# A two-layer hybrid encoder: tokens laid in blocks of 8 columns, and the wide products of the feed-forward put in front of the narrow ones

## The chip, the cores and the metric

The kernel runs on one core of a Trainium2 chip. The metric is the device time in microseconds, the median of several runs of the same program; beside it there is one profiled execution, whose trace gives start and duration of each instruction. TensorE (PE) makes the matrix products and writes them to PSUM; VectorE (DVE), ScalarE (ACT) and GpSimd (POOL) work on the results; SyncE (SP) and, for a few, GpSimd issue the DMA transfers.

## What is computed

512 tokens of width 1024 lie on a grid of 8 rows and 64 columns. Two layers are applied, then a final RMS norm:

```python
for l in range(DEPTH):                                    # DEPTH = 2
    x = x + hybrid_mixer(rms_norm(x, norm_mix[l]), ...)   # neighbourhood attention || grouped-query attention
    x = x + memory_cross_attention(rms_norm(x, ...), rms_norm(mem, ...), ...)
    x = x + conv_ffn(rms_norm(x, norm_ffn[l]), w_up[l], conv_w[l], conv_b[l], w_down[l])
return rms_norm(x, norm_final)

def conv_ffn(h, w_up, conv_w, conv_b, w_down):
    u = h @ w_up                                          # (512, 2 * 2816)
    up = jnp.pad(u, ((0, 0), (1, 1), (0, 0)))
    u = up[:, :-2] * conv_w[0] + up[:, 1:-1] * conv_w[1] + up[:, 2:] * conv_w[2] + conv_b
    gate, val = jnp.split(u, 2, axis=-1)
    return (jax.nn.silu(gate) * val) @ w_down
```

The neighbourhood attention looks at a window of all 8 rows by 16 columns around each token. The convolution of the feed-forward, in contrast, runs over the tokens in their natural order, which is row by row: token n stands in row n // 64 and column n % 64, and its neighbours are tokens n - 1 and n + 1.

## The kernel before, in words

**Layout.** The activations are held transposed, as eight tiles xT[0..7] of 128 channels by 512 tokens, in fp32. The host lays the tokens out column by column (position = column * 8 + row), so that a window of columns is a run of positions. Every matrix product is computed in parts: an operand is split into hi (rounded to the product's format) and lo (the rest), and a product is made of hi x hi, hi x lo and lo x hi (mm3, L925). gemm_T (L931) sums such triples over the 128-row chunks of the contraction; each single product is one PE.matmul at L101 (a counting wrapper), so all of them have this line in the profile.

**Stages of a layer.** Input projection and both attentions are woven together (weave and Filler), then come the output projection, the memory attention and the feed-forward. A Norm object closes a stage: close (L1017) adds the product in PSUM to xT[c], copies the sum back to xT[c], writes hi of the next operand from PSUM (operand, L1025), then lo, then the square for the norm's statistic (L1034). The statistic becomes a row of factors that is spread over the partitions by four small products (row_bank, L991) and copied to the tile rep (row_rep, L998).

**The feed-forward.** The 22 units of 128 gate and 128 value channels are worked through in the order of sequence() (L836), which interleaves the units with rows of the down projection of the group before (GROUPS holds 6, 6, 5 and 5 units; PLAIN is 6).
- Units 0 to 5 are plain: up_project (L1843, up_first L1848 for the first ones) makes 24 products of 512 columns for each side, gate and value, from the operand tiles of the norm, ffn.ops; up_finish (L1869) multiplies by rep and calls convolve.
- Units 6 to 21 use a two-by-two fast multiplication with fewer block products. scale_tokens (L1908) makes the normalised tokens xn with one DVE instruction for each xT[c]; token_sums and split_form (L1915, L1930) make seven forms of 4 x 256 columns, hi and lo side by side in 512. up_forms (L1945) calls product() (L1952) seven times for a unit. A call makes, for each of four chunks, one product of the weight's hi with hi and lo together (512 columns, "wide") and one of the weight's lo with hi alone (256 columns, "narrow"):

```python
for k in range(4):
    i = 4 * part + k
    both = xform[form][k // 2][:, k % 2]
    PE.matmul(bank, wh[:, i], both, ...)
    PE.matmul(bank[:, halves[0]], wl[:, i], both[:, halves[0]], ...)
```

- convolve (L1874) makes the middle tap and the bias on ACT, then the outer taps on DVE (L1891). In the column order, the neighbour of a token lies 8 positions away, except that the neighbour of the last column lies at the start of the next row; so each outer tap is two instructions, one over 504 columns and one over 7. SiLU, the product of gate and value and the split into hi and lo follow.
- down (L1993) adds a row of the down projection to xT[m] (L1999). After the last group, down_closing (L2001) closes into the first norm of the next layer, or down_last (L2018) ends the kernel: the last group's first two units are added to xT[m] at L2028, and of the rest one half of the tokens is finished transposed and the other half in rows of tokens.

**The order of the work.** SP's transfers keep the order in which the program writes them. The instructions of PE, ACT, DVE and POOL are put into a new order by a planner (Order, L347): it simulates the program with written-down costs for each instruction (Step.times, L300) and buffer counts (SLOTS, L199), gives every instruction a due time from the products that need it, replays the order several times with random delays and keeps the best of 12 rounds; the random numbers have a fixed seed. A change of any instruction anywhere can so change the order of others in the whole kernel.

Of the kernel before, what the change touches and what calls it, by code (L numbers as in the profile page):

```python
# [11 lines left out]
F32 = mybir.dt.float32  # L12
F32R = mybir.dt.float32r
AF = mybir.ActivationFunctionType
# [5 lines left out]
P = 128  # L20
# [3 lines left out]
GW = 64  # L24
ROWS = 8
NB = S // P
KC = D // P
HD = 64
MEMN = 256
# [61 lines left out]
class Counted(Free):  # L91
# [4 lines left out]
    def matmul(self, out, lhsT, rhs, **k):  # L96
        n = 1
        for d in rhs.shape[1:]:
            n *= d
        self.ns += max(107.0, (n + 32) / 2.4)  # L100
        return self.engine.matmul(out, lhsT, rhs, **k)  # L101


class PartsView:
# [579 lines left out]
def encoder_kernel(ctx: ExitStack, tc: tile.TileContext, t: dict, out: bass.AP):  # L684
# [151 lines left out]
    def sequence():  # L836

        before = None  # L840
        for g, (j0, nj) in enumerate(GROUPS):
            row = 0
            for j in range(j0, j0 + nj):
                to = 0 if g == 0 else min(KC, 2 * (j - j0) + 1) if j < j0 + nj - 1 else KC
                rows, row = range(row, to), to
                if j < PLAIN:
                    yield "up", j, None
                    continue
                yield "gate", j, None
                if before is not None:  # L850
                    yield "val", before, None
                yield "sums", j, None
                if len(rows) > 1:
                    yield "down", g - 1, rows[:1]
                    rows = rows[1:]
                yield "diffs", j, None
                before = j
                if j == NF - 1:
                    yield "val", j, None
                if rows:  # L860
                    yield "down", g - 1, rows
# [133 lines left out]
                      start=True, stop=True)  # L995
        return pr

    def row_rep(rstd, n, tag, bufs, copy):  # L998

        pr = row_bank(rstd, n)  # L1000
        rep = tpool.tile([P, n * P], F32, tag=tag, name=nm(tag), bufs=bufs)
        copy(rep, pr[:, : n * P])
        return rep, pr[:, : n * P]

    class Norm:
# [8 lines left out]
        def gain(self, c):  # L1014
            return par[:, self.l, self.gcol + c : self.gcol + c + 1]

        def close(self, c, pm):  # L1017


            DVE.tensor_add(pm, pm, xT[c])  # L1020
            DVE.tensor_copy(xT[c], pm)
            self.operand(c, src=pm)
            self.square(c)

        def operand(self, c, act=ACT, src=None, dve=DVE, hi_only=False, lo_only=False):  # L1025
            src = xT[c] if src is None else src
            g = self.gain(c)
            hi, lo = self.ops[c]
            e = None if lo_only else act.activation(hi, src, AF.Copy, scale=g)
            if not hi_only:  # L1030
                dve.scalar_tensor_tensor(lo, src, g, f(hi), op0=ALU.mult, op1=ALU.subtract)
            return e
# [39 lines left out]
            POOL.tensor_tensor(self.rstd, v, mhalf[:, :nb], op=ALU.pow)  # L1072

        def spread(self, copy=ACT.copy):
            self.rep, self.psum = row_rep(self.rstd, self.n // P, "rep", 1, copy)

    def split_psum(hi, lo, ps, scale=None):
        if scale is None:
# [119 lines left out]
    for l in range(DEPTH):  # L1198
# [639 lines left out]


        ffn = nn  # L1840
        acts = {}

        def up_project(j, side):  # L1843
            pm = ps_s() if side else ps_mm()
            gemm_T(pm, get_w(("up", j, side)), ffn.ops, range(KC), 0, KC - 1)
            return pm

        def up_first():  # L1848


            ws, us = [], []
            for side in range(2):
                ws.append(get_w(("up", 0, side)))
                us.append(ps_mm())
                gemm_T(us[side], ws[side], ffn.ops, range(KC - 1), 0, KC - 1)
            for side in range(2):
                gemm_T(us[side], ws[side], ffn.ops, [KC - 1], 0, KC - 1)
                if side == 0:
                    ffn.stat()
            us1 = [up_project(1, 0)]  # L1860
            ffn.spread()
            up_finish(0, us)
            us1.append(up_project(1, 1))
            up_finish(1, us1)
# [9 lines left out]
        def convolve(j, us):  # L1874
            cs = []
            for side in range(2):
                ch = side * NF + j
                u = us[side]
                if side and j >= PLAIN:
                    w = [minus[:, l, i, j : j + 1] for i in range(3)]  # L1880
                else:
                    w = [par[:, l, CW + i * 2 * NF + ch : CW + i * 2 * NF + ch + 1] for i in range(3)]
                cc = tmp()
                ACT.activation(cc, u, AF.Identity, bias=par[:, l, CB + ch : CB + ch + 1], scale=w[1])
                for wi, dst, src in (
                    (w[0], slice(8, S), slice(0, S - 8)),
                    (w[0], slice(1, 8), slice(S - 8, S - 1)),
                    (w[2], slice(0, S - 8), slice(8, S)),
                    (w[2], slice(S - 8, S - 1), slice(1, 8)),
                ):  # L1890
                    DVE.scalar_tensor_tensor(cc[:, dst], u[:, src], wi, cc[:, dst], op0=ALU.mult, op1=ALU.add)  # L1891
                cs.append(cc)
            ACT.activation(us[0], cs[0], AF.Silu)
            DVE.tensor_mul(us[0], us[0], cs[1])
            acts[j] = rpair()
            split_psum(*acts[j], us[0])
            if j == NF - 1 and l + 1 < DEPTH:
                turn_table(AF.Exp)
# [9 lines left out]
        def scale_tokens():  # L1908


            xn.extend(rtile((2, S), F32) for _ in range(4))
            for c in range(KC):
                DVE.scalar_tensor_tensor(xn[c // 2][:, c % 2], xT[c], ffn.gain(c), ffn.psum, op0=ALU.mult, op1=ALU.mult)

        def token_sums():  # L1915

# [28 lines left out]
        def up_forms(j):  # L1945
# [6 lines left out]
            def product(bank, name, part, form, start=True):  # L1952
                if name not in ws:
                    ws[name] = get_w((name, j))
                wh, wl = ws[name]
                for k in range(4):
                    i = 4 * part + k
                    both = xform[form][k // 2][:, k % 2]
                    PE.matmul(bank, wh[:, i], both, start=start and k == 0, stop=False, skip_group_check=True)
                    PE.matmul(bank[:, halves[0]], wl[:, i], both[:, halves[0]], start=False, stop=k == 3, skip_group_check=True)  # L1960

            def total(dst, bank):
                DVE.tensor_reduce(dst, bank.rearrange("p (n c) -> p c n", n=2), axis=AX.X, op=ALU.add)  # L1963
# [29 lines left out]
        def down(g, rows):  # L1993
            j0, nj = GROUPS[g]
            ops = [acts[j] for j in range(j0, j0 + nj)]
            for m in rows:
                pm = ps_mm()
                gemm_T(pm, get_w(("down", g, m)), ops, range(nj), 0, nj - 1)
                DVE.tensor_add(xT[m], xT[m], pm)  # L1999

        def down_closing(g):  # L2001
            j0, nj = GROUPS[g]
            ops = [acts.pop(j) for j in range(j0, j0 + nj)]
            opened = []
            for m in range(KC):
                if m < 3:
                    opened.append((ps_mm(), get_w(("down", g, m))))
                    gemm_T(*opened[m], ops, range(nj - 1), 0, nj - 1)
            for m in range(KC):
                if m < 3:  # L2010
                    pm, w = opened[m]
                    gemm_T(pm, w, ops, [nj - 1], 0, nj - 1)
                else:
                    pm = ps_mm()
                    gemm_T(pm, get_w(("down", g, m)), ops, range(nj), 0, nj - 1)
                nn.close(m, pm)

        def down_last():  # L2018

            parts = [{j: acts.pop(j) for j in range(j0, j0 + nj)} for j0, nj in LAST]  # L2020
            gain = rtile((2, S), F32)
            SP.dma_start(gain, t["gain"])
            for m in range(KC):
                if m % 2 == 0:
                    w = get_w(("down", "a", m // 2))
                pm = ps_mm()
                gemm_T(pm, w, list(parts[0].values()), range(LAST[0][1]), 0, LAST[0][1] - 1, slice(P * (m % 2), P * (m % 2) + P))
                DVE.tensor_add(xT[m], xT[m], pm)  # L2028

            js, ws = list(parts[1]), {}  # L2030

# [115 lines left out]
def _rope_tables():  # L2147


    tok = np.arange(S)  # L2150
    col, row = tok // ROWS, tok % ROWS
    pos = np.stack([row, col], axis=-1).astype(np.float32)
    nf = HD // 4
    inv = np.float32(10000.0) ** (-np.arange(nf, dtype=np.float32) / np.float32(nf))
# [13 lines left out]
def _bias_index():  # L2168


    q = np.arange(P)
    k = np.arange(256)
    ro = (k % ROWS)[None, :] - (q % ROWS)[:, None] + ROWS - 1
    ci = np.empty((P, 3, 256), np.int64)
    for y, (q0, k0) in enumerate(((0, 0), (16, 8), (48, 32))):
        qc, kc = q0 + q // ROWS, k0 + k // ROWS
        s0 = np.clip(qc - 8, 0, GW - 16)[:, None]
        dc = kc[None, :] - qc[:, None]
        ci[:, y] = np.where((kc >= s0) & (kc < s0 + 16), dc + 15, 31)
    return np.broadcast_to(ro[:, None, :], ci.shape), ci  # L2180


# [41 lines left out]
```

## Time and profile before

| what | us |
|---|---|
| median of 3 runs | 1304.17 (1303.88 to 1304.24) |
| the profiled execution's own time | 1304.26 |
| its span, first to last instruction | 1302.5 |
| DVE busy | 916.0 |
| ACT busy | 776.6 |
| POOL busy | 857.7 |

An engine's busy time is the union of its instructions' times. A row of a group reads: line, engine, operation, the names out<-in, partitions x elements and type, count, then the busy time in us and the mean of one in ns, then the engine's idle time just before them and what ended it. A row of the timeline reads: start in us, us, engine, line, operation, names, shape, count of merged instructions. In the chain of waits a piece reads: start in us, us, engine and line, count. In the table of waits: who waited for whom, then us in total, times, and the longest. The durations of TensorE's products overlap; the time from start to start is what a product costs in a stream.

### The profile page before, as it was taken

To read this page: it belongs to the slowest core of one execution; us is meant where nothing else is said; L and a number is where in the kernel's file an instruction comes from. 1 tells how busy PE (TensorE), PEld (TensorE's weight loads), DVE (VectorE), ACT (ScalarE), POOL (GpSimd) and SP (SyncE) were. 2 spreads that over 40 slices of the span, in tenths; PEclk is the share of its full clock that TensorE was granted. 3 is DMA by queue.
4 is the path that set the end of the run, shared out by engine and by line. 5 is a ranking of instruction groups with operands and counts; after the bars stand their busy time and mean duration, and the time that the engine had idled before them with its cause. 6 is when DMAs were issued, how large, how long until landed. Compare 5 with 4: busy or idle time off the path is not lost.

```text
span 1302.5 us, 19581 instructions
## 1 busy us (share of the span) xinstructions
PE 1292.3 (99%) x6699; PEld 1096.4 (84%) x6699; DVE 916.0 (70%) x1869; ACT 776.6 (60%) x1463; POOL 857.7 (66%) x650
## 2 busy tenths in 40 slices
PE   9999999999999999999999999999999999999997
PEld 8888888888888888888888888888888888888887
DVE  6559877665996685676735698776759966666675
ACT  6667866565564554454636687775645545545454
POOL 3657966728667776776746579766466766767673
PEclk9999999999999999999999999999999999999999
DMA  9734599597787789687555435986872454555541
GB/s 289 211 108 121 160 262 203 168 211 199 186 192 204 207 230 234 189 234 212 157 152 172 144 84 185 253 191 214 186 170 85 130 158 134 163 157 150 149 138 65
DMA packets 287426, 229.68 MB, mean 176 GB/s; under 512 B 7648, under 2 KB 243680, under 8 KB 287328
## 3 DMA queue, kind: packets, MB, share of 16 engines
q1 hardware_dynamic: 270016, 194.49, 49.7%
q0 software_dynamic: 16896, 33.56, 14.6%
q8 instruction: 53, 0.87, 0.3%
q10 hardware_dynamic: 416, 0.39, 0.1%
q14 instruction: 45, 0.37, 0.1%
HBM read 218.45 MB, written 69.21 MB: 221 GB/s over the span
## 4 chain that ended last, share of the span: by engine, by line
PE 95%; DVE 3%; ACT 1%; issue 1%; POOL 0%; POOLq 0%; DVEq 0%; ACTq 0%
PE mm L101 69%; PE sc L101 18%; PE tr L101 4%; PE tr L1586 2%; PE tr L1431 1%; PE tr L1780 1%; DVE t L1891 0%; DVE r L1080 0%; DVE sc L1403 0%; PE tr L1501 0%; DVE r L1129 0%; DVE t L1456 0%; DVE t L1489 0%; ACT r L1079 0%; ACT t L1409 0%
## 5 line engine op out<-in xcount | busy, mean ns | idle before, releaser
L790 POOL TENSOR_TENSOR lo<-raw,hi 128x512 fp32r<-128x512 f32 (+3 forms) x325 | 567.0, 1761 | 280.6 <-ACT hi L789 224.1
L789 ACT CAST hi<-raw 128x1024 fp32r<-128x1024 f32 (+3 forms) x361 | 287.8, 814 | 274.4 <-issue 71.3
L101 PE MATMUL mm<-r,hi 128*128 128x512 f32 (+1 forms) x1344 | 432.8, 390 | 0.0
L101 PEld LDWEIGHTS mm<-r,hi 128*128 128x128 f32 x1344 | 246.4, 188 | 49.8
L101 PE MATMUL mm<-r,lo 128*128 128x512 f32 (+1 forms) x832 | 286.5, 347 | 0.0
L101 PE MATMUL mm<-xg,hi 128*128 128x512 f32 x800 | 262.2, 394 | 0.6 <-DVE t L1963 0.6
L101 PE MATMUL mm<-xg,lo 128*128 128x512 f32 (+1 forms) x528 | 177.9, 337 | 0.0
L101 PEld LDWEIGHTS mm<-r,lo 128*128 128x128 f32 x832 | 156.4, 188 | 22.6 <-POOL lo L790 0.5
L101 PEld LDWEIGHTS mm<-xg,hi 128*128 128x128 f32 x800 | 148.6, 188 | 31.9 <-DVE t L1963 1.0
L101 PE MATMUL sc<-xg,hi 128*128 128x512 f32 x352 | 116.3, 395 | 0.0
L101 PE MATMUL mm<-hi,xg 128*128 128x512 f32 (+1 forms) x384 | 111.2, 360 | 0.0
L101 PEld LDWEIGHTS mm<-xg,lo 128*128 128x128 f32 x528 | 99.4, 188 | 12.2
L1086 POOL TENSOR_SCALAR t<-t,s 128x512 f32<-128x512 f32 (+1 forms) x112 | 67.2, 623 | 45.6 <-DVE s L1570 22.2
L101 PE MATMUL sc<-xg,lo 128*128 128x256 f32 (+1 forms) x240 | 79.4, 332 | 0.0
L1982 POOL TENSOR_TENSOR t<-t 128x256 f32<-128x256 f32 x32 | 42.4, 1324 | 56.1 <-ACT t L1981 55.2
L101 PEld LDWEIGHTS sc<-xg,hi 128*128 128x128 f32 x352 | 66.1, 189 | 14.5 <-ACT xg L78 0.4
L101 PEld LDWEIGHTS mm<-hi,xg 128*128 128x128 f32 x384 | 68.0, 189 | 9.1 <-DVE r L1280 0.2
L101 PE MATMUL sc<-r,r 128*128 128x256 f32 (+1 forms) x352 | 74.4, 330 | 0.0
L1989 DVE TENSOR_TENSOR sc<-mm,t 128x256 f32<-128x256 f32 x32 | 13.8, 433 | 79.2 <-ACT t L1988 79.2
L101 PE MATMUL sc<-r,hi 128*128 128x512 f32 x192 | 68.7, 398 | 0.0
L101 PE MATMUL mm<-lo,xg 128*128 128x512 f32 (+1 forms) x192 | 68.6, 357 | 0.0
L790 DVE TENSOR_TENSOR lo<-raw,hi 128x1024 fp32r<-128x1024 f32 (+1 forms) x36 | 44.2, 1229 | 33.8 <-ACT hi L789 33.5
(222 smaller groups left out, 2438.3 us busy)
## 6 DMA issues: line engine op xcount, KB each, us to landing
raw<-in_w_up SPq DMA_DIRECT2D x56, 512.0 KB, 4.5
dr_sums<-in_w_up SPq DMA_DIRECT2D x16, 1024.0 KB, 8.0
dr_diffs<-in_w_up SPq DMA_DIRECT2D x16, 1024.0 KB, 7.6
raw<-dr_sums SPq DMA_DIRECT2D x32, 512.0 KB, 4.1
raw<-dr_diffs SPq DMA_DIRECT2D x32, 512.0 KB, 4.1
raw<-in_w_in SPq DMA_DIRECT2D x25, 512.0 KB, 4.8
raw<-in_w_down SPq DMA_DIRECT2D x32, 384.0 KB, 3.7
raw<-in_w_mem_kv SPq DMA_DIRECT2D x16, 512.0 KB, 4.4
```

The source lines that it names most:

```text
L101: return self.engine.matmul(out, lhsT, rhs, **k)
L789: act.copy(hi[:, k], raw[:, k])
L790: (POOL if eng[0] == "P" else DVE).tensor_sub(lo[:, k], raw[:, k], f(hi)[:, k])
L1086: eng.tensor_scalar(e, e, sums[:, col : col + 1], 1.0, op0=ALU.mult, op1=ALU.mult)
L1431: PE.transpose(tr[:, (2 * i + c) * P : (2 * i + c + 1) * P], es[j][:, i, c * P : (c + 1) * P], ident)
L1586: PE.transpose(tr[:, k * P : (k + 1) * P], es[j][:, k * P : (k + 1) * P], ident)
L1780: PE.transpose(tr[:, (2 * c + i) * P : (2 * c + i + 1) * P], e[:, i, c * P : (c + 1) * P], ident)
L1982: POOL.tensor_add(vc, vc, u2)
L1989: DVE.tensor_add(ch, ah, l4)
```

## The change

1. **Layout.** The host lays the tokens in blocks of 8 columns: position = block * 64 + row * 8 + column in the block. Tables, bias index and the final reshape follow it (host only). The attentions run in this order. 
2. **The feed-forward runs in the natural order.** Two views make the passage between the orders: crossed() reads a row of 512 as 8 x 8 runs of 8 elements in the other order, runs() gives the plain row the same shape. The plain units read hi and lo through crossed() as the moving operand (576 products); the residual adds, the spread of rep, the closes into the next layer and the adds of down_last read one side through crossed(). scale_tokens becomes one ACT and one DVE instruction for each xT[c], and down_last writes its sums to new tiles z.
3. **One instruction for each outer tap**, over 511 columns, in place of two.
4. **In product()** the four wide products come first and the four narrow ones behind them.
5. sequence() can yield down rows for a plain unit.

```diff
+def runs(v):
+    return v.rearrange("p (a b e) -> p a b e", a=GROUPS_OF_COLS, b=ROWS)
+def crossed(v):
+    return v.rearrange("p (a b e) -> p b a e", a=ROWS, b=ROWS)
...
                 if j < PLAIN:
                     yield "up", j, None
+                    if rows:
+                        yield "down", g - 1, rows
                     continue
...
-        copy(rep, pr[:, : n * P])
+        copy(runs(rep), crossed(pr)) if turned else copy(rep, pr[:, : n * P])
...
+            if by_row:
+                DVE.tensor_add(runs(pm), runs(pm), crossed(xT[c]))
+                DVE.tensor_copy(runs(xT[c]), crossed(pm))
+            else:
+                DVE.tensor_add(pm, pm, xT[c])
+                DVE.tensor_copy(xT[c], pm)
+            self.operand(c, src=pm, by_row=by_row)
...
+            if by_row:
+                e = act.activation(runs(hi), crossed(src), AF.Copy, scale=g)
+                src = xT[c]
...
         ffn = nn
+        by_row = [tuple(map(crossed, v)) for v in ffn.ops]
...
-            gemm_T(pm, get_w(("up", j, side)), ffn.ops, range(KC), 0, KC - 1)
+            gemm_T(pm, get_w(("up", j, side)), by_row, range(KC), 0, KC - 1)
...
-                for wi, dst, src in (
-                    (w[0], slice(8, S), slice(0, S - 8)),
-                    (w[0], slice(1, 8), slice(S - 8, S - 1)),
-                    (w[2], slice(0, S - 8), slice(8, S)),
-                    (w[2], slice(S - 8, S - 1), slice(1, 8)),
-                ):
+                for wi, dst, src in ((w[0], slice(1, S), slice(0, S - 1)), (w[2], slice(0, S - 1), slice(1, S))):
                     DVE.scalar_tensor_tensor(cc[:, dst], u[:, src], wi, cc[:, dst], op0=ALU.mult, op1=ALU.add)
...
-                DVE.scalar_tensor_tensor(xn[c // 2][:, c % 2], xT[c], ffn.gain(c), ffn.psum, op0=ALU.mult, op1=ALU.mult)
+                v = xn[c // 2][:, c % 2]
+                ACT.activation(runs(v), crossed(xT[c]), AF.Copy, scale=ffn.gain(c))
+                DVE.tensor_mul(runs(v), runs(v), crossed(ffn.psum))
...
+                both = [xform[form][k // 2][:, k % 2] for k in range(4)]
                 for k in range(4):
-                    i = 4 * part + k
-                    both = xform[form][k // 2][:, k % 2]
-                    PE.matmul(bank, wh[:, i], both, start=start and k == 0, stop=False, skip_group_check=True)
-                    PE.matmul(bank[:, halves[0]], wl[:, i], both[:, halves[0]], start=False, stop=k == 3, skip_group_check=True)
+                    PE.matmul(bank, wh[:, 4 * part + k], both[k], start=start and k == 0, stop=False, skip_group_check=True)
+                for k in range(4):
+                    PE.matmul(bank[:, halves[0]], wl[:, 4 * part + k], both[k][:, halves[0]], start=False, stop=k == 3,
+                              skip_group_check=True)
...
-                DVE.tensor_add(xT[m], xT[m], pm)
+                DVE.tensor_add(runs(xT[m]), runs(xT[m]), crossed(pm))
...
-                nn.close(m, pm)
+                nn.close(m, pm, True)
...
+            z = [v[:, i] for v in (rtile((2, S), F32) for _ in range(4)) for i in range(2)]
...
-                DVE.tensor_add(xT[m], xT[m], pm)
+                DVE.tensor_add(runs(z[m]), crossed(xT[m]), runs(pm))
+                xT[m] = z[m]
...
-    col, row = tok // ROWS, tok % ROWS
+    col, row = tok // GW * ROWS + tok % ROWS, tok // ROWS % ROWS
...
-        "xT": a["x"].reshape(ROWS, GW, D).transpose(2, 1, 0).reshape(D, S),
+        "xT": a["x"].reshape(ROWS, GROUPS_OF_COLS, ROWS, D).transpose(3, 1, 0, 2).reshape(D, S),
```

More of the change, by code (lines that the diff above doesn't have):

```diff
@@ L26 @@
 NB = S // P
+GROUPS_OF_COLS = GW // ROWS
 KC = D // P
@@ L996, in row_bank, with row_rep @@
         return pr
-    def row_rep(rstd, n, tag, bufs, copy):
+    def row_rep(rstd, n, tag, bufs, copy, turned):
         pr = row_bank(rstd, n)
         rep = tpool.tile([P, n * P], F32, tag=tag, name=nm(tag), bufs=bufs)
-        copy(rep, pr[:, : n * P])
+        copy(runs(rep), crossed(pr)) if turned else copy(rep, pr[:, : n * P])
         return rep, pr[:, : n * P]
@@ L1015, in gain, with close, operand @@
             return par[:, self.l, self.gcol + c : self.gcol + c + 1]
[L1017 to L1022, printed above, removed]
+        def close(self, c, pm, by_row=False):
+            if by_row:
[5 more added lines that the diff above has]
+            self.operand(c, src=pm, by_row=by_row)
             self.square(c)
-        def operand(self, c, act=ACT, src=None, dve=DVE, hi_only=False, lo_only=False):
+        def operand(self, c, act=ACT, src=None, dve=DVE, hi_only=False, lo_only=False, by_row=False):
             src = xT[c] if src is None else src
@@ L1028, in operand @@
             hi, lo = self.ops[c]
-            e = None if lo_only else act.activation(hi, src, AF.Copy, scale=g)
+            if by_row:
+                e = act.activation(runs(hi), crossed(src), AF.Copy, scale=g)
+                src = xT[c]
+            else:
+                e = None if lo_only else act.activation(hi, src, AF.Copy, scale=g)
             if not hi_only:
@@ L1074, in spread @@
         def spread(self, copy=ACT.copy):
-            self.rep, self.psum = row_rep(self.rstd, self.n // P, "rep", 1, copy)
+            self.rep, self.psum = row_rep(self.rstd, self.n // P, "rep", 1, copy, self.gcol == G_FFN)
     def split_psum(hi, lo, ps, scale=None):
@@ L1854, in up_first @@
                 us.append(ps_mm())
-                gemm_T(us[side], ws[side], ffn.ops, range(KC - 1), 0, KC - 1)
+                gemm_T(us[side], ws[side], by_row, range(KC - 1), 0, KC - 1)
             for side in range(2):
-                gemm_T(us[side], ws[side], ffn.ops, [KC - 1], 0, KC - 1)
+                gemm_T(us[side], ws[side], by_row, [KC - 1], 0, KC - 1)
                 if side == 0:
@@ L2172, in _bias_index @@
     k = np.arange(256)
-    ro = (k % ROWS)[None, :] - (q % ROWS)[:, None] + ROWS - 1
+    (qr, qc), (kr, kc) = ((v // ROWS % ROWS, v // GW * ROWS + v % ROWS) for v in (q, k))
+    ro = kr[None, :] - qr[:, None] + ROWS - 1
     ci = np.empty((P, 3, 256), np.int64)
     for y, (q0, k0) in enumerate(((0, 0), (16, 8), (48, 32))):
[L2176 to L2179, printed above, removed]
+        s0 = np.clip(q0 + qc - 8, 0, GW - 16)[:, None]
+        dc = k0 + kc[None, :] - (q0 + qc)[:, None]
+        ci[:, y] = np.where((k0 + kc >= s0) & (k0 + kc < s0 + 16), dc + 15, 31)
     return np.broadcast_to(ro[:, None, :], ci.shape), ci
@@ L2222 @@
     y = np.concatenate([y[0].reshape(D, HALF).T, y[1].reshape(HALF, D)])
-    return np.ascontiguousarray(y.reshape(GW, ROWS, D).transpose(1, 0, 2)).reshape(1, S, D)
+    return np.ascontiguousarray(y).reshape(1, S, D)
```

## The prediction

> **What bounds the kernel now.** I read the profile's page first, then the table of what TensorE waited for, then the chain of waits in order of time and the timeline of TensorE, and last the groups of DVE instructions by shape. The profiled execution took 1304.26 us (span 1302.5 us and 1.76 us around it), 0.09 us over the median of the runs, 1304.17 us, so a sum made against it carries over to the median. A measurement of this kernel can tell about 0.2%, 2.6 us, from no change.
>
> ```profile
> PE 1292.3 (99%) x6699; PEld 1096.4 (84%) x6699; DVE 916.0 (70%) x1869; ACT 776.6 (60%) x1463; POOL 857.7 (66%) x650
> PEclk9999999999999999999999999999999999999999
> PE 95%; DVE 3%; ACT 1%; issue 1%; POOL 0%; POOLq 0%; DVEq 0%; ACTq 0%
> ```
> ```profile
> PE tr L101 <- POOL ident masks.py:199: 1.4, 1, 1.4
> PE tr L1431 <- DVE r L1297: 0.8, 1, 0.8
> PE mm L101 <- DVE t L1963: 0.6, 1, 0.6
> PE mm L101 <- DVE t L1457: 0.4, 2, 0.2
> PE tr L101 <- DVE r L1080: 0.3, 1, 0.3
> ```
>
> TensorE is busy for 99% of the span at the full clock and makes 95% of the chain that ended last. All its waits together are 3.5 us, and 0.9 us of them (L1963, L1080) lie in the feed-forward. So the time is the number of products times the pitch at which they start, plus a start and a tail of a few us. Work taken from DVE, ACT or POOL can gain no more than a part of those 3.5 us; the pitch is what the change must be held against. The pitch is read from start to start, since the 390 ns of one product in the groups overlap the next.
>
> ```profile
> 326.73 5.44 PE mm L101 x24
> ```
> ```profile
> 574.49 0.40 PE L101 MATMUL mm<-r,hi 128*128 128x512 f32 x1
> 574.72 0.28 PE L101 MATMUL mm<-r,lo 128*128 128x256 f32 x1
> 574.84 0.40 PE L101 MATMUL mm<-r,hi 128*128 128x512 f32 x1
> ...
> 581.08 0.28 PE L101 MATMUL sc<-r,lo 128*128 128x256 f32 x1
> 581.20 0.64 PE L101 MATMUL mm<-r,hi 128*128 128x512 f32 x2
> ```
> ```profile
> 698.06 1.12 PE L101 MATMUL sc<-r,r 128*128 128x256 f32 x8
> 699.01 0.63 PE L101 MATMUL mm<-xg,hi 128*128 128x512 f32 x2
> ...
> 700.85 0.39 PE L101 MATMUL mm<-xg,lo 128*128 128x512 f32 x1
> ```
>
> An up projection of 24 wide products (512 columns) takes 5.44 us: **226.7 ns** for each wide one in an unbroken stream. A run of eight narrow ones (256 columns) takes 699.01 - 698.06 = 0.95 us: about **119 ns** each. Alone, one wide and one narrow would so cost 346 ns. Where product() alternates them, 19 pairs run from 574.49 to 581.20: 6.71 / 19 = **353.2 ns** a pair. Alternation costs 7 ns a pair over the two streams.
>
> **The change part by part.**
>
> *Wide before narrow in product().* One unit of up_forms makes 7 calls of product() with 4 wide and 4 narrow each; 16 units in each of 2 layers make 224 calls. Now a call costs 4 x 353.2 = 1413 ns. Short runs of narrow and wide in turn stand in the attention, most plainly here:
>
> ```profile
> 126.11 0.64 PE L101 MATMUL mm<-r,r 128*128 128x256 f32 x4
> 126.59 0.40 PE L101 MATMUL mm<-hi,xg 128*128 128x512 f32 x1
> 126.83 0.39 PE L101 MATMUL mm<-lo,xg 128*128 128x512 f32 x1
> 127.05 0.39 PE L101 MATMUL mm<-hi,xg 128*128 128x512 f32 x1
> 127.28 0.64 PE L101 MATMUL mm<-r,r 128*128 128x256 f32 x4
> 127.75 0.40 PE L101 MATMUL mm<-hi,xg 128*128 128x512 f32 x1
> ...
> 128.45 0.60 PE L1431 MATMUL tr<-ident,t 128*128 128x128 f32 x4
> ```
>
> Four narrow and three wide take 1.17 us, twice (126.11 to 127.28, 127.28 to 128.45). A fourth wide adds 227 to 233 ns (the stream's pitch, or that of the second triple, 0.70 / 3), so a grouped call is 1397 to 1403 ns: 10 to 16 ns less. I take 13: 224 x 13 = **2.9 us**. The ends: nothing, if the extra 7 ns belong to each narrow product and not to each change of width; and 30 ns a call, 6.7 us, if grouped calls reach the two streams, 4 x 226.7 + 4 x 119 = 1383 ns.
>
> The down rows behind a call carry a debt too:
>
> ```profile
> 407.80 0.64 PE L101 MATMUL mm<-r,hi 128*128 128x512 f32 x2
> ...
> 411.94 0.39 PE L101 MATMUL mm<-xg,hi 128*128 128x512 f32 x1
> ```
>
> Right after an alternating stretch, 18 wide products take 411.94 - 407.80 = 4.14 us, 60 ns over 18 x 226.7. Right after the run of eight narrow ones (fence above), 8 wide take 700.85 - 699.01 = 1.84 us, 27 ns over. A grouped call ends in narrow ones like the second case, so up to 33 ns go at each of the places where down rows follow a call: by sequence() 8 in each of three groups, and the closing, 25 a layer, 50 in all, so 0 to 1.7 us. I take the middle, **0.9 us**. Together the order is worth 3.8 us, between 0 and 8.4.
>
> The narrow products wait for nothing new: they read the same weight tiles, hi and lo fetched by one get_w, and the same forms as the wide ones ahead of them. The last product of a call, on which the evictions wait, ends where it ended, less those 13 ns.
>
> *Crossed moving operand.* 6 units x 2 sides x 24 products x 2 layers = 576 wide products now read hi and lo through a view of 64 runs of 8 elements. No row of before has such a moving operand. The nearest are the value products, which read two runs of 128, against narrow ones over one run:
>
> ```profile
> L101 PE MATMUL sc<-r,r 128*128 128x256 f32 x224 | 34.1, 287 | 0.0
> L101 PE MATMUL mm<-r,r 128*128 128x256 f32 x128 | 18.6, 285 | 0.0
> ```
>
> Two runs take 285 ns, one run 287: no price, so I take **0**. The upper end is my estimate from the stream: one column's time, 226.7 / 512 = 0.44 ns, lost at each of 63 breaks is 28 ns a product, 576 x 28 = 16.1 us. A gain I exclude, as no product becomes shorter. [...]
>
> *One instruction for each outer tap.*
>
> ```profile
> L1891 DVE SCALAR_TENSOR_TENSOR t<-tr,par,t 128x504 f32<-128x504 f32 x64 | 47.0, 734 | 2.5 <-ACT t L1884 2.5
> L1891 DVE SCALAR_TENSOR_TENSOR t<-tr,par,t 128x7 f32<-128x7 f32 x64 | 13.8, 215 | 0.0
> L1963 DVE TENSOR_REDUCE t<-mm 128x256 f32<-128x512 f32 x64 | 44.0, 688 | 17.8 <-PE mm L101 17.5
> L1561 DVE TENSOR_REDUCE s<-sc 128x1 f32<-128x512 f32 x64 | 42.3, 683 | 4.7 <-PE sc L101 4.4
> L1913 DVE SCALAR_TENSOR_TENSOR r<-xT,par,tr 128x512 f32<-128x512 f32 x16 | 11.3, 738 | 0.0
> L1999 DVE TENSOR_TENSOR xT<-xT,mm 128x512 f32<-128x512 f32 x48 | 32.8, 683 | 8.9 <-PE mm L101 8.9
> L1029 ACT ACTIVATE xg<-mm,par 128x512 fp32r<-128x512 f32 x32 | 21.5, 683 | 6.1 <-DVE xT L1021 5.8
> ```
>
> 22 units x 2 sides x 2 layers x 2 = 176 short taps of 215 ns go, 37.8 us of DVE; the long ones grow from 504 to 511 columns, 734 / 504 x 7 = 10 ns each, 1.8 us. That frees 36 us of an engine that is 70% busy. On TensorE's path it is worth at most the 0.9 us of DVE waits in the feed-forward; as every engine's order is planned anew over the whole kernel, it can as well be minus 0.9. I take 0. Its cover is the next unit's products, 24 x 226.7 ns in a plain one, 28 pairs of 353 ns in one with forms; if that were gone, a unit's chain would be shorter by its four short taps, 0.86 us.
>
> *Reads across the two orders.* The residual adds (L1999, 48, and 8 in down_last), the 8 closes at the layer's boundary with their copy and hi, and the two spreads keep their counts and only read crossed. The price is zero by L1963, which reads PSUM a bank's half apart at every element in 688 ns, where L1561 reads 512 in a row in 683. In the closes lo now reads xT and no longer PSUM, behind the copy in DVE's own order; the adds and the next products queue behind it as before. Eight x tiles more in down_last (four buffers of 21) come when the forms are dead. scale_tokens replaces 16 instructions of 738 ns on DVE by 16 on ACT (683 as L1029) and 16 on DVE (683 as L1999): ACT gains 10.9 us over the kernel, 5.5 in each layer, inside a stage of 12 projections x 5.44 = 65 us before the first form is read. Price zero; without that cover 5.5 us a layer. The new line in sequence() yields nothing: group 0 has no rows, and all units below PLAIN are in it. No DMA is added or moved, and no queue is passed.
>
> **Sum:** 1304.3 - 2.9 - 0.9 + 0 + 0 = **1300.5 us**.
>
> **The rivals.**
>
> *The order is worth nothing.* The mechanism would be a fixed cost of each product whatever stands beside it; the pitch then sums the same in any order, and the time stays at **1304.3**. For it: the trace has stretches without any debt, the 24 wide of an up projection, and few places with short runs in turn. Against it: 353.2 against 346 ns, and the 60 ns of debt behind alternation, both many times repeated. [...]
>
> *The crossed reads slow TensorE.* Place: the first 65 us of each feed-forward. Price: 28 ns on 576 products, 16.1 us, less the 3.8 us of the order: **1316.6**. It decides from 6.6 ns a product (3.8 us / 576), 3% of one. For it: no row shows 64 runs, and TensorE has no slack to hide it. Against it: 285 against 287 ns for two runs.
>
> *The full gain.* If the change of width is all that costs and a run of four is enough, 8.4 us go: **1295.9**. The row at 126.59 leans to it (three wide in 0.69 us, 9 ns over the stream); the one at 127.75 (0.70 us) does not.
>
> **How the numbers follow.** Forecast 58%, order worthless 22%, crossed reads dear 12%, full gain 8%. The forecast's own range is 1298.5 to 1302.5. The range over all runs from **1297.0** (most of the full gain; 5% lie below) to **1305.0** (order worthless, and 0.9 us more of DVE waits; 14% lie above). Faster by over 0.2%, below 1301.6: nearly all of the forecast and the full gain, 0.60. Within 0.2%: the rest of the forecast and the worthless order, 0.27. Slower: the crossed reads and a bad new plan, 0.13.
>
> **What would show it.** In the profile after: eight products of one product() call (4 x 128x512, then 4 x 128x256) in about 1.40 us, against 1.41; the up projections still 5.44 us for 24, and if they show 5.6 or more the crossed reads are dear; no 128x7 taps, DVE near 880 us, TensorE's waits still a few us. I am wrong if grouped calls keep 1.41 us, or if TensorE's waits in the feed-forward exceed 2 us.

## The result and the profile after

| kernel | median us | ratio to before (95% interval) |
|---|---|---|
| before | 1304.11 | 1 |
| changed | 1320.23 (1319.72 to 1321.65) | 1.0124 (1.0111 to 1.0136) |

The change makes the kernel slower by 16.1 us. The profiled execution of the changed kernel took 1319.94 us, its span 1318.1 us, 15.6 us more than before.

The page of the changed kernel, the busy times and the head of the chain that ended last:

```profile
PE 1308.2 (99%) x6699; PEld 1098.8 (83%) x6699; DVE 907.6 (69%) x1693; ACT 784.9 (60%) x1479; POOL 858.2 (65%) x650
PE 96%; DVE 2%; ACT 1%; issue 1%; POOL 0%; DMA 0%; POOLq 0%; SPq 0%; DVEq 0%; ACTq 0%
```

TensorE makes the same 6699 products and is busy 15.9 us longer. So the time is in the products themselves, and what TensorE waited for says the same:

```profile
PE tr L102 <- POOL ident masks.py:199: 1.4, 1, 1.4
PE tr L1452 <- DVE r L1318: 0.8, 1, 0.8
PE tr L1607 <- DVE r L1318: 0.4, 1, 0.4
PE mm L102 <- POOL lo L801: 0.3, 1, 0.3
PE mm L102 <- DVE t L1478: 0.2, 1, 0.2
PE sc L102 <- ACT xg L79: 0.2, 1, 0.2
```

3.3 us against 3.5 before; the two waits on DVE in the feed-forward are gone. The chain in order of time (start us, us, engine and line, count) names the place:

```profile
328.94 6.32 PE mm L102 x24
335.26 6.32 PE sc L102 x24
...
979.14 6.32 PE mm L102 x24
```

These are the up projections of the plain units in both layers: 24 products in **6.32 us**, 263.3 ns each, where it was 5.44 us and 226.7 ns. They are the products that read hi and lo crossed, and 36.6 ns on 576 of them would be 21.1 us. The timeline shows that the first unit pays less:

```profile
306.36 0.40 PE L102 MATMUL mm<-xg,lo 128*128 128x512 f32 x1
306.59 0.64 PE L102 MATMUL mm<-xg,hi 128*128 128x512 f32 x2
...
313.36 0.40 PE L102 MATMUL mm<-xg,lo 128*128 128x512 f32 x1
```

From 306.36 to 313.36 stand ten triples, 30 products at 233.3 ns. With all starts of the crossed products summed against 226.7 ns, the price is **18.7 us**.

The grouped product() calls, in the timeline of TensorE:

```profile
447.26 1.09 PE L102 MATMUL tr<-r,hi 128*128 128x512 f32 x4
448.19 0.63 PE L102 MATMUL tr<-r,lo 128*128 128x256 f32 x4
448.66 1.09 PE L102 MATMUL mm<-xg,hi 128*128 128x512 f32 x4
...
451.47 1.09 PE L102 MATMUL sc<-r,hi 128*128 128x512 f32 x4
452.40 0.64 PE L102 MATMUL sc<-r,lo 128*128 128x256 f32 x4
452.87 0.40 PE L102 MATMUL mm<-r,hi 128*128 128x512 f32 x1
```

Four calls from 447.26 to 452.87: 5.61 us, **1402 ns** a call against 1413. Summed over all other products, the starts lie 8.2 us over the two streams (226.7 and 120 ns), and 11.0 us before: 2.8 us gained. The sum closes: 18.7 - 2.8, and 0.2 us less in the table of waits, make 15.7 us, where the span shows 15.6.

### The profile page after: what moved, and what is told of

The parts are those of the page before. It is cut to its first block, busy times and chain, and to the rows that moved or that the text cites. A ratio compares the mean times of both kernels' runs of the same rounds, so it can differ in the third digit from the quotient of the medians.

```text
span 1318.1 us, 19401 instructions
## 1 busy us (share of the span) xinstructions
PE 1308.2 (99%) x6699; PEld 1098.8 (83%) x6699; DVE 907.6 (69%) x1693; ACT 784.9 (60%) x1479; POOL 858.2 (65%) x650
## 4 chain that ended last, share of the span: by engine, by line
PE 96%; DVE 2%; ACT 1%; issue 1%; POOL 0%; DMA 0%; POOLq 0%; SPq 0%; DVEq 0%; ACTq 0%
PE mm L102 69%; PE sc L102 19%; PE tr L102 4%; PE tr L1607 2%; PE tr L1452 1%; PE tr L1801 1%; DVE r L1318 0%; PE tr L1522 0%; DVE sc L1424 0%; DMA xT<-in_xT 0%; DVE t L1510 0%; DVE r L1101 0%; ACT hi L800 0%; DVE r L1150 0%; DVE t L1477 0%
## 5 line engine op out<-in xcount | busy, mean ns | idle before, releaser
L102 PE MATMUL mm<-r,hi 128*128 128x512 f32 (+1 forms) x1344 | 409.4, 389 | 0.0
L102 PE MATMUL mm<-r,lo 128*128 128x512 f32 (+1 forms) x832 | 256.0, 347 | 0.0
L102 PE MATMUL mm<-xg,hi 128*128 128x512 f32 x800 | 245.4, 401 | 0.0
L102 PEld LDWEIGHTS mm<-r,lo 128*128 128x128 f32 x832 | 147.3, 188 | 25.7 <-DVE lo L801 0.8
L102 PE MATMUL mm<-xg,lo 128*128 128x512 f32 (+1 forms) x528 | 150.6, 345 | 0.0
L102 PE MATMUL sc<-xg,hi 128*128 128x512 f32 x352 | 110.0, 410 | 0.2 <-ACT xg L79 0.2
L102 PEld LDWEIGHTS mm<-xg,lo 128*128 128x128 f32 x528 | 91.0, 190 | 18.9
L1100 ACT CAST r<-tr 128x512 fp32r<-128x512 f32 x80 | 46.1, 587 | 40.9 <-DVE tr L1911 30.0
L801 DVE TENSOR_TENSOR lo<-raw,hi 128x1024 fp32r<-128x1024 f32 (+1 forms) x36 | 47.7, 1327 | 28.4 <-ACT hi L800 28.4
L102 PE MATMUL sc<-xg,lo 128*128 128x256 f32 (+1 forms) x240 | 66.9, 345 | 0.0
```

Source lines behind the costliest of these rows:

```text
L801: (POOL if eng[0] == "P" else DVE).tensor_sub(lo[:, k], raw[:, k], f(hi)[:, k])
L1100: ACT.copy(hi, ps)
```

## The experiments

My first theory after the result: the crossed read of the moving operand is the loss, and the order of products gains some 3 us. The rivals were that the order is worth nothing, and that the loss lies in the crossed adds and closes or in the new plan. "Before" in each run is the kernel before on the same chip, 1304.3 to 1304.4 us. In the four runs that change the view of the moving operand, the tokens of the plain units come out in a wrong order; nothing is left out. Each of these four times is a single execution.

**The order of products alone.** The loop of product() from the change, in the kernel before:

```diff
+                both = [xform[form][k // 2][:, k % 2] for k in range(4)]
                 for k in range(4):
...
+                    PE.matmul(bank, wh[:, 4 * part + k], both[k], ...)
+                for k in range(4):
+                    PE.matmul(bank[:, halves[0]], wl[:, 4 * part + k], both[k][:, halves[0]], ...)
```

> The kernel before, with the wide products of product() in front of the narrow ones and nothing else. Theory: the order pays what the trace of the changed kernel shows in the two stretches of forms, 1.4 us in each layer and a little in the down rows, so 3.0 us less, 1301.1 us, with one call of product() in about 1.40 us. Rival: the order is worth nothing and what the changed kernel gained came from the lighter DVE (its waits fell by 0.9 us): 1304.1 us.

Measured: 1303.81 us, ratio 0.9996 (0.9987 to 1.0005), the time of the rival. But its mechanism is not the rival's. The starts lie 8.5 us over the two streams in place of 11.0, so the pitch did pay 2.5 us. It went to waits; the table of TensorE's waits in this run has lines that were not there before:

```profile
PE sc L101 <- DVE lo L790: 0.9, 1, 0.9
...
PE mm L101 <- DVE lo L790: 0.7, 2, 0.3
PE tr L1501 <- DVE r L1080: 0.4, 1, 0.4
```

L790 is the lo of a weight's split, on DVE. Counted as all gaps of over 45 ns beyond the pitch, after the start's first 6.5 us, waits and the restarts behind them grew from 7.7 to 10.3 us. The level of this count hangs on which restarts are taken in; only its differences are used here.

**The crossed read alone, and the length of its runs.** In the kernel before, only the view that the up products read:

```diff
         ffn = nn
+        turned = [tuple(v.rearrange("p (a b e) -> p b a e", a=8, b=8) for v in vs) for vs in ffn.ops]
...
-            gemm_T(pm, get_w(("up", j, side)), ffn.ops, range(KC), 0, KC - 1)
+            gemm_T(pm, get_w(("up", j, side)), turned, range(KC), 0, KC - 1)
```

> The kernel before, with nothing changed but that the 576 up products of the plain units read hi and lo as 64 runs of 8 elements, 256 bytes apart; the tokens of those units come out in another order, so the output differs. Theory: the crossed read alone costs TensorE 18.7 us, 36.6 ns on most products: 1322.8 us and 6.32 us for 24 products. Rival: the loss comes from what else the change touched (the closes, the adds, a new plan), and the read itself is cheap: below 1308 us and 5.5 us for 24.

The other three have (a, b) of (8, 4), (8, 16) and (4, 4), which give runs of 16, 4 and 32 elements.

> As the run with runs of 8, but the view has 32 runs of 16 elements (64 bytes each, 256 bytes apart). Theory of a price for each break: 31 breaks in place of 63, so half of 18.7 us, 1313.4 us and 5.87 us for 24 products. Rival, a price for each 64 bytes that are only half used: nothing is half used here, so no price, 1304.1 us and 5.44 us. Second rival, a price for the three-dimensional pattern whatever its runs: 1322.8 us and 6.32 us.

> As the runs of 8 and of 16, with 128 runs of 4 elements (16 bytes). Theory of a price for each break, with the 0.58 ns a break of the steady products with 64 runs (36.6 ns over 63): 127 breaks cost 74 ns a product, 42 us in all: 1346 us. Rival, a price for each 64 bytes opened and not used up: 128 openings in place of 64 also doubles the price, but then the runs of 16 would have been free, and they cost 12.7 ns a product. Second rival, a limit that is reached once and stays: 1323 us, as with runs of 8.

> The same with 16 runs of 32 elements (128 bytes). Theory of a price for each break, by the 0.41 ns of the runs of 16 (12.7 ns over 31): 15 breaks cost 6 ns a product, 3.5 us: 1307.9 us and 5.58 us for 24 products. Rival: long runs hide the break, 1304.4 us and 5.44 us.

The chain of each of the four runs, runs of 4, 8, 16 and 32 in this order, has for 24 up products:

```profile
331.39 6.63 PE mm L101 x24
```
```profile
329.25 6.32 PE mm L101 x24
```
```profile
327.81 5.75 PE mm L101 x24
```
```profile
327.19 5.60 PE mm L101 x24
```

| run of | runs | time us | over before, us | a product in the steady stretch, ns | over 226.7, ns | ns a break |
|---|---|---|---|---|---|---|
| 4 (16 bytes) | 128 | 1332.63 | 28.3 | 276.2 | 49.5 | 0.39 |
| 8 | 64 | 1323.18 | 18.8 | 263.3 | 36.6 | 0.58 |
| 16 | 32 | 1311.22 | 6.8 | 239.6 | 12.9 | 0.42 |
| 32 (128 bytes) | 16 | 1307.59 | 3.3 | 233.3 | 6.6 | 0.44 |

With runs of 8 the read alone costs 18.8 us, as the theory said, and no close, add or plan of the change is in this kernel. The price falls with the number of breaks and is still there with runs of 32. A price for 64 bytes left half used is refuted by the runs of 16 (64 bytes each, and 12.9 ns a product), a price for the three-dimensional pattern as such by the spread of all four (6.6 to 49.5 ns). A break costs about 0.4 ns, close to one column's 0.44 ns (226.7 / 512); only the runs of 8 stand out, and their two pitches (233.3 over 30 products of the first unit, 263.3 in the steady stretch) show that something beside the count of breaks sets it. I expected 1346 us for runs of 4 by the 0.58 ns; at 0.4 ns it would have been 1334. Two things were not taken apart: with 512 columns a larger count of breaks is also a shorter run, and the runs lie 256 bytes apart in three of the views (512 in the one with runs of 32), so what another distance costs is not shown.

**The passage made in the closes.** The changed kernel, where x is copied and hi is written crossed out of PSUM in the closes before and after the feed-forward, so that TensorE reads whole rows; scaling, spread and adds of the down rows as before.

```diff
             DVE.tensor_add(pm, pm, xT[c])
             if by_row:
                 DVE.tensor_copy(runs(xT[c]), crossed(pm))
...
-                nn.close(m, rows[m][0])
+                nn.close(m, rows[m][0], True)
...
-            gemm_T(pm, get_w(("up", j, side)), by_row, range(KC), 0, KC - 1)
+            gemm_T(pm, get_w(("up", j, side)), ffn.ops, range(KC), 0, KC - 1)
```

> The changed kernel, but the passage into the natural order is made once, in the closes (the copy of x and the write of hi read PSUM crossed), so that the up products read whole rows; the adds of the down rows, the spread and the scaling of the tokens are those of before. Theory: the crossed read was the whole loss, so 18.7 us go from 1320.2: 1301.5 us, and 5.44 us for 24 up products; a gain over the kernel before of about 3 us is left. Rival: a part of the loss lies in the crossed adds and closes or in the plan: over 1306 us.

Measured: 1303.95 us, ratio 0.9998 (0.9989 to 1.0007). The up products are back at 5.44 us, so the loss is gone. The gain of the order is there in the pitch (8.2 us over the streams) and lost again in waits (10.4 us). The groups of DVE and TensorE's waits of this run show a cause that I had not expected:

```profile
L1051 DVE SCALAR_TENSOR_TENSOR xg<-xT,par,xg 128x512 fp32r<-128x512 f32 x24 | 36.3, 1535 | 1.5 <-ACT xg L1046 1.5
L1051 DVE SCALAR_TENSOR_TENSOR xg<-mm,par,xg 128x512 fp32r<-128x512 f32 x12 | 8.8, 743 | 1.5 <-ACT xg L1049 1.5
```
```profile
PE mm L102 <- DVE xg L1051: 1.3, 2, 0.9
```

The lo of a close that reads x from SBUF takes 1535 ns in the mean, the one that reads PSUM 743, in the same kernel. TensorE waits for it at the head of both feed-forwards: the gaps of over 45 ns from 304.5 to 308.2 us and from 945.5 to 950.0 us make 2.9 us, where the kernel before has none; the waits of the whole kernel grew by 2.7. The length of the lo goes with what POOL does meanwhile. One of the 24 and the POOL instruction beside it:

```profile
638.80 1.75 POOL L1068 TENSOR_TENSOR t<-t,t 128x512 f32<-128x512 f32 x1
639.93 1.18 DVE L1051 SCALAR_TENSOR_TENSOR xg<-xT,par,xg 128x512 fp32r<-128x512 f32 x1
```

POOL's ends at 640.55, and the lo 0.56 us later. Of the 24 that read x from SBUF, 17 start with 0.3 to 2.3 us of a POOL instruction still ahead, and each lasts that rest and 546 to 553 ns more. Two start just as one begins and take 1.86 and 1.87 us; the five with less than 0.2 us ahead take 734 to 740 ns. The 16 that read PSUM all start while POOL works, and take 737 to 752 ns.

**The passage made in the evictions.** The memory attention's output and, in the first layer, the last group's activations are written in the other order when they leave PSUM; the closes add x crossed and read PSUM for lo, as before.

```diff
             if by_row:
                 DVE.tensor_add(runs(pm), runs(pm), crossed(xT[c]))
             else:
                 DVE.tensor_add(pm, pm, xT[c])
             DVE.tensor_copy(xT[c], pm)
             self.operand(c, src=pm)
...
-            split_psum(*mo[h], po)
+            split_psum(*map(runs, mo[h]), crossed(po))
...
+            if l + 1 < DEPTH and j >= GROUPS[-1][0]:
+                split_psum(*map(runs, acts[j]), crossed(us[0]))
+            else:
+                split_psum(*acts[j], us[0])
```

> The version with the passage in the closes made anew: the memory attention's output and, in the first layer, the last group's activations are written in the other order when they are evicted from PSUM, so the closes only add x crossed, and lo reads PSUM as in the kernel before. Theory: the version with the passage in the closes lost what the order gives (2.8 us in the two feed-forwards) to waits, 3.1 us of them for lo in the close, which reads x from SBUF there and takes 1586 ns in the median in place of 740 when POOL reads SBUF too; here these waits go, and about 2.8 us are gained: 1301.6 us. Rival: the waits are a matter of the plan's luck, any new plan has some, and the sum stays within 1 us of 1304.4.

Measured: **1301.32 us**, ratio 0.9978 (0.9969 to 0.9987). It is faster than both kernels. Page, chain and groups of this run:

```profile
PE 1289.5 (99%) x6699; PEld 1095.9 (84%) x6699; DVE 901.2 (69%) x1693; ACT 775.1 (60%) x1463; POOL 855.4 (66%) x650
```
```profile
326.83 5.44 PE mm L102 x24
```
```profile
L1051 DVE SCALAR_TENSOR_TENSOR xg<-mm,par,xg 128x512 fp32r<-128x512 f32 x32 | 23.6, 744 | 8.4 <-ACT xg L1049 8.4
```

The up products are whole again, all lo of the closes take 740 to 744 ns, the starts lie 8.0 us over the streams and the waits are 7.7 us, as in the kernel before. So 3.0 us are gained in the pitch and none is given back.

**Order and taps apart, and the plan's luck.** The version with the passage in the evictions, once with alternating products again and once with another seed of the planner; the kernel before with another seed; the order alone with two others.

```diff
-ROUNDS, REPLAYS, MARGIN, SHARES, STRETCH, SEED = 12, 4, 100.0, (0.0, 0.0, 0.5, 1.0, 2.0), 500, 4
+ROUNDS, REPLAYS, MARGIN, SHARES, STRETCH, SEED = 12, 4, 100.0, (0.0, 0.0, 0.5, 1.0, 2.0), 500, 5
```

> The version with the passage in the evictions (1301.3 us), but with wide and narrow products alternating again in product(): the natural order and the single outer taps alone. Theory: the order of products is what pays, 2.8 us in the two feed-forwards, and the lighter DVE only keeps that gain from going to waits: 1304.1 us. Rival: the lighter DVE is the gain (the order alone gave nothing, 1303.8 us): 1301.5 us.

> The version with the passage in the evictions, with another seed for the planner. Theory: with DVE lighter by 36 us any plan finds room, so the gain stays: 1301.8 us. Rival: the gain was a lucky plan: 1303.8 us.

> The kernel before with another seed for the planner (5 in place of 4), so that the same instructions are put in another order. Theory: the plan alone moves the time by some 2 us, because TensorE's waits do (7.7 us in all in the kernel before, start and joints included, 10.3 us with the order of products changed): 1306 us, as the kept seed is a good one. Rival: the plan hardly matters, within 0.5 us of 1304.4, and then the order of products brought its waits by itself.

> The order of products alone, with the planner's seed 5; the kernel before took 1304.85 us with this seed. Theory: the 2.5 us that grouped products save went to waits by the plan of that seed; with this one a part stays: 1302.8 us. Rival: the grouped order brings its waits by itself, as the split of the weights, on DVE beside POOL, comes too late: 1304.3 us again.

> The same with seed 6: 1302.8 us by the first theory, 1304.3 us by the second.

| products | layout | seed | time us | ratio (95% interval) | waits us |
|---|---|---|---|---|---|
| alternating | before | 4 | 1304.3 | 1 | 7.7 |
| alternating | before | 5 | 1304.85 | 1.0005 (0.9995 to 1.0015) | 8.5 |
| grouped | before | 4 | 1303.81 | 0.9996 (0.9987 to 1.0005) | 10.3 |
| grouped | before | 5 | 1302.59 | 0.9988 (0.9977 to 0.9998) | 9.0 |
| grouped | before | 6 | 1301.98 | 0.9984 (0.9974 to 0.9994) | 8.5 |
| alternating | evictions | 4 | 1306.45 | 1.0016 (1.0007 to 1.0026) | 9.7 |
| grouped | evictions | 4 | 1301.32 | 0.9978 (0.9969 to 0.9987) | 7.7 |
| grouped | evictions | 5 | 1301.86 | 0.9981 (0.9971 to 0.9992) | 8.6 |

Grouped against alternating, with the same seed and layout: -0.5, -2.3 and -5.1 us. The pitch gives 2.5 to 3.4 us each time, and the waits add 2.6 and 0.5 us or take 2.0. The seed alone moves the waits of the grouped order between 8.5 and 10.3 us, so a part of its loss with the kept seed was the plan's luck; as its three plans wait 8.5 us or more and the two alternating ones 7.7 and 8.5, it is not shown that the order brings none. The order of products alone comes to 1302.59 and 1301.98 us with seeds 5 and 6, near the 1301.32 and 1301.86 of the version with the evictions, so with a better plan the order alone gives most of that version's gain. The natural order with its single taps gave nothing by itself: with alternating products it took 2.1 us more than before, though DVE was busy 18 us less (page of that run):

```profile
PE 1294.0 (99%) x6699; PEld 1096.3 (84%) x6699; DVE 898.3 (69%) x1693; ACT 776.2 (59%) x1463; POOL 858.7 (66%) x650
```

That this version's 2 us of waits are luck as well is likely by the table, but only one seed of it was run.

## Why the prediction was wrong

*What bounds the kernel*: right. The whole change is in TensorE's pitch, and waits moved by less than 3 us in any run.

*Crossed moving operand*: here it failed. "Two runs take 285 ns, one run 287: no price, so I take **0**." The row has one break, and its time is the duration of one product, which overlaps the next, not the pitch; from start to start these products take about 119 ns with two runs and with one, and a break of 0.4 ns can't be seen in either. Nothing in the row says what 63 breaks cost. 63 breaks cost 36.6 ns in the steady stretch, 18.7 us in all, and the single edit reproduced it (18.8 us). My upper end, one column at each break and 16.1 us, had the right form and was 2.6 us short. With TensorE's 99% on the path the doubt belonged in the sum, not in a rival at 12%: no row of before shows more than two runs, so the value was open between the ends. The rival's place and mechanism came true, its 1316.6 us missed the result by 3.6 us, and the sign given for it in the prediction ("if they show 5.6 or more") came at 6.32.

*Wide before narrow*: right in mechanism, a little too large. Forecast 13 ns a call and 0.9 us in the down rows, 3.8 us together; measured 11 ns a call (1402 against 1413), 2.5 to 3.4 us together in the pitch; the down rows were not measured apart. The rival that the order is worth nothing is refuted by the pitch and by two of three pairs in time, though the pair with the kept seed and the layout of before gave its number. The full gain of 8.4 us did not come: a call stays over the streams' 1383 ns.

*One instruction for each tap*: the taps of 511 columns take 743 to 745 ns, 10 ns more as forecast, and 176 instructions went. DVE's busy time fell by 8.4 us and not by 36. A part is that short taps overlap: in the timeline of DVE before, they start 0.13 to 0.14 us apart, not 0.215:

```profile
458.63 0.21 DVE L1891 SCALAR_TENSOR_TENSOR t<-sc,minus,t 128x7 f32<-128x7 f32 x1
458.77 0.22 DVE L1891 SCALAR_TENSOR_TENSOR t<-tr,par,t 128x7 f32<-128x7 f32 x1
458.90 0.73 DVE L1891 SCALAR_TENSOR_TENSOR t<-sc,minus,t 128x504 f32<-128x504 f32 x1
```

So they cost some 23 us when only the stretch is counted that each adds to DVE's busy time, and as the longer taps grew by 4.6 us, 18.7 went. Counted so, instructions that read two tensors from SBUF took back most of it: the lo of the forms 7.7 us, that of the closes 4.1, that of the weights 3.3. All others together took 4.8 less. The largest group of the forms' lo, before and after:

```profile
L1943 DVE TENSOR_TENSOR r<-r,r 128x512 fp32r<-128x512 f32 x12 | 15.2, 1283 | 0.0
L1962 DVE TENSOR_TENSOR r<-r,r 128x512 fp32r<-128x512 f32 x12 | 21.2, 1793 | 0.0
```

For the time it makes nothing, as forecast: DVE has 2% of the chain that ended last, and TensorE's waits fell by 0.2 us.

*Reads across the two orders* on DVE and ACT: free, as forecast (adds of down rows 683 ns before and after; in the closes of the changed kernel the add takes 696 ns crossed and 693 to 696 plain, the copy 681 and 686 to 687, hi on ACT 679 and 682). What I passed over stands in the same sentence: "lo now reads xT and no longer PSUM". In the group of the changed kernel it shows:

```profile
L1052 DVE SCALAR_TENSOR_TENSOR xg<-xT,par,xg 128x512 fp32r<-128x512 f32 x8 | 10.3, 1301 | 0.0
```

1301 ns where PSUM as source takes 749. Here it is eight times at the layer's boundary and is covered (of all waits for L1052 one shows, 0.2 us of a weight load); in the version with the passage in the closes it stood at the head of the feed-forward and cost waits.

## What to carry to other kernels

Where TensorE is busy all the time, price every change of its moving operand's access pattern by its breaks, by these runs some 0.4 to 0.6 ns for each break of an fp32 read, and let ACT or DVE do the reordering when they evict PSUM, where it was free (the memory attention's eight evictions lie in a group of 28 that took 583 ns on ACT and 683 on DVE in the mean, against 582 and 684 in the kernel before). A row that hardly shows the new thing is no proof of a zero price; with no slack to hide it, its upper end belongs in the forecast. A gain of a few us in the pitch can be eaten by the luck of a planned order: judge it by the starts, or by more than one seed.

## What the runs showed of the hardware

- A moving operand of 512 fp32 columns in 16, 32, 64 and 128 runs costs 6.6, 12.9, 36.6 and 49.5 ns over the 226.7 of one run. With 64 runs TensorE also held 233.3 ns over 30 products, in a stretch of the first unit, and went to 263.3 after eight small products in between, in the changed kernel as in the run with the view alone; the twelve products ahead of that stretch took 257 (302.80 to 305.88 us in the changed kernel). Why there are two pitches stays open.
- The width of the products beside a product counts: a wide one takes 226.7 ns and a narrow one 119 in a stream of its own, 346 together, and a pair in alternation takes 353.2; in the kernel before, 18 wide ones right behind an alternating stretch took 60 ns more than the stream, 8 behind a run of narrow ones 27 ns more.
- A DVE instruction with both tensors in SBUF took 1301 and 1535 ns in the mean where the same one from PSUM took 743 to 749. In the version with the passage in the closes, 17 of the 24 lasted until the POOL instruction beside them ended (a sum of squares or the lo of a weight, both read from SBUF) and 546 to 553 ns more. No run took POOL's work away, so that POOL is the cause was not shown.
